# A price for the port that VectorE and GpSimd share, in the planner of a two-layer decoder trunk

## The chip, the cores and the metric

The kernel runs on one core of a Trainium2 chip. The metric is the device time of one execution in microseconds, taken as the median of several runs. The profiled execution has a time of its own, and inside it a span, from the first to the last instruction.

## The reference

The input is 1024 tokens of width 1024 in float32. Two layers follow each other, each of the form norm, mixer, residual, norm, gated feed-forward, residual:

```python
for layer in range(DEPTH):
    h = rms_norm(x, attn_norm[layer])
    if layer % 2 == 0:
        z = h @ w_in_e[i]                       # 1024 -> 2072 columns
        a_out = nsa_attention(...)              # compressed, selected and window branch, 8 heads
        b_out = swa_sink_attention(bq, bk, bv, sinks[i])   # window of 128, 8 heads
        x = x + concat([a_out, b_out]) @ w_out_e[i]
    else:
        q, k, v = split(h @ w_qkv_o[j])         # 16 heads
        x = x + dilated_attention(rope(q), rope(k), v) @ w_out_o[j]
    h = rms_norm(x, ffn_norm[layer])
    gate, up = split(h @ w_gate_up[layer])
    x = x + (silu(gate) * up) @ w_down[layer]   # hidden width 2816
return rms_norm(x, final_norm)
```

## The kernel before

The tokens are worked on in two halves of 512. Nearly every matrix product is done as three products of a high and a low part of each operand, which gives float32 accuracy from TensorE's faster formats. So each weight tile costs, beside its load, one cast on ScalarE (the high part, `splits`) and one subtraction on VectorE or GpSimd (the low part, `lows`), and each tile of attention weights costs the same (`weights`: exponential and cast on ScalarE, subtraction on VectorE or GpSimd).

The dense products (projections, output projections, feed-forward) are a list of 355 jobs that run in order on TensorE, accumulating in the banks pD. Jobs 0 to 29 are the input projection of layer 0, 30 to 116 the output projection and feed-forward of its first half and the projection of layer 1, 117 to 206 the same for the second half, 207 to 283 and 284 to 354 the two halves of layer 1. Attention runs beside them: scores in pS whose row maxima VectorE takes (`maxima`; the maxima MR are transposed by a TensorE row `pS<-ident,MR`), transposed scores in pT (`st_unit`), weights in the tiles PH, and sums in pO (`pv_unit`). 

The order of all of this isn't written by hand. Every piece of work is a generator (a task) that says which engine its next step needs, and a planner, `Kernel.run`, always advances the task whose step can start first by the planner's own clocks. One clock stands for each engine: "p" TensorE, "v" VectorE, "a" ScalarE, "g" GpSimd, "s" the DMA queue of SyncE. Each operation that is issued is priced by `account`, which sets the clock of its engine and the time from which its result is seen. The prices are `COST = {"v": (68, 1.043), "a": (50, 0.836), "g": (60, 2.2)}`, a start and an amount for each column, in nanoseconds. The order in which the planner issues is the order in which each engine's queue then runs; on the chip nothing is reordered, and real waits are set by semaphores.

Two choices lean on these clocks. `attend` lets a unit of attention go ahead of its share when the next dense row could not start in time:

```python
if n + 1 > ph["n"] * (self.done - lo) / (hi - lo):
    d = self.start(self.dense_at)
    if d <= self.clk["p"] + 250.0:
        return INF
```

And `vg` gives an elementwise operation between SBUF tiles to VectorE, unless GpSimd would be done sooner by the two clocks:

```python
v = max(self.clk["v"], self.now) + COST["v"][0] + COST["v"][1] * n
v += self.o.queue * self.waiting("v")
g = max(self.clk["g"], self.now) + COST["g"][0] + COST["g"][1] * n
return self.nc.vector if v + slack < g else self.nc.gpsimd
```

All instructions are issued through one helper, so the profile gives them all the same line, L242, and they are told apart by their tiles: S stands for the work tiles in SBUF, SM and MR for small ones, pD, pS, pT, pO for banks of PSUM.

Of the kernel before, what the change touches and what calls it, by code (L numbers as in the profile page):

```python
# [69 lines left out]
def cols(ap):  # L70
    return int(np.prod(ap.shape[1:]))


class Buf:


    def __init__(self, arena, place, raw):
        self.arena, self.place, self.raw, self.live = arena, place, raw, True
# [180 lines left out]
class Kernel:  # L259
    def __init__(self, nc, tc, ctx, io):  # L260
        self.tc, self.io = tc, io
        self.clk = {e: BEGIN for e in "pvags"}
        self.info, self.scope, self.wire, self.pe = {}, 0.0, 0.0, 0.0
        self.nc = Core(self, nc)
        pool = lambda name, **kw: ctx.enter_context(tc.tile_pool(name=name, bufs=1, **kw))
        self.const, self.sb = pool("const"), pool("sb")
        self.ps = pool("ps", space=bass.MemoryType.PSUM)
        self.dram = pool("dram", space=bass.MemoryType.DRAM)
        self.n = 0
        arena = lambda name, n, shape, dt: Arena(name, n, self.sb, shape, dt, self.info)  # L270
        self.S4 = arena("S4", N4, [P, 1032], F32R)
        self.S2 = arena("S2", N2, [P, HT], F32)
        self.PH = arena("PH", NPH, [P, HT], F16)
        self.OS = arena("OS", 3, [P, HB, 65], F32)
        self.OG = arena("OG", NOG, [P, HB, 66], F32)
        self.MR = arena("MR", 20, [P, HB], F32R)
        self.SM = arena("SM", NSM, [P, 8], F32)
        self.NM = arena("NM", 3, [HB, P], F32R)
        self.TM = arena("TM", 3, [P, HB, 64], F32)
        bank = lambda name, n, first: Arena(name, n, self.ps, [P, 512], F32, self.info, "bank", first)  # L280
        self.pS, self.pT, self.pO, self.pD = bank("pS", 2, 0), bank("pT", 2, 2), bank("pO", 1, 4), bank("pD", 3, 5)
        self.tasks, self.seq = [], 0
        self.have = {}
        self.done, self.dense_at = 0.0, None
        self.o, self.rnd, self.zone = SimpleNamespace(**ORDER), random.Random(0), 0
# [9 lines left out]
    def account(self, key, name, a, kw):  # L295

        aps = [x for x in list(a) + list(kw.values()) if hasattr(x, "tensor")]
        outs = [kw["out"] if "out" in kw else aps[0]]
        if "accum_out" in kw:
            outs.append(kw["accum_out"])  # L300
        ins = [x for x in aps if not any(x is o for o in outs)]
        t = self.clk[key]
        for x, rd in [(x, True) for x in ins] + [(x, False) for x in outs]:
            i = self.info.get(x.tensor.name)
            if i is not None:
                if rd or key != "s" or i[2] != "s":
                    t = max(t, i[1] + SELF[key] if i[2] == key else i[0])
                if not rd:
                    t = max(t, i[3])
        if key == "s":  # L310
            n = int(np.prod(a[0].shape)) * 4
            self.clk["s"] = t + 600.0
            self.last = t
            self.wire = max(self.wire, t + 1300.0) + n / 330.0
            end = see = self.wire + 700.0
        else:
            if key == "p":

                n = (4.0 if name == "matmul" else 2.0) if a[1].dtype == F32 else 1.0
                cost = max(cols(a[0]) / 2.4, 22.0) * n * (2.0 if t < COLD else 1.0) + 2.5  # L320
                t = max(t, self.pe + (26.0 if a[1].dtype in (F16, BF) else 107.0 * (n if n > 2 else 1.0)))
                self.pe = t
            else:
                c = COST[key]
                cost = c[0] + (1.45 if name == "affine_select" else c[1]) * max(cols(x) for x in aps if len(x.shape) > 1)
                if key == "a" and not any(x.tensor.name[:2] in ("pS", "pT", "pO", "pD") for x in aps):
                    cost += 43.0 if name == "copy" else 136.0
            end = t + cost
            see = end + LAT[key]
            self.clk[key] = end  # L330
            self.last = t
        for x in ins:
            i = self.info.setdefault(x.tensor.name, [0.0, 0.0, "", 0.0])
            i[3] = max(i[3], see)
        for x in outs:
            i = self.info.setdefault(x.tensor.name, [0.0, 0.0, "", 0.0])
            i[0], i[1], i[2] = max(i[0], see), max(i[1], end), key
        self.scope = max(self.scope, see)
# [2357 lines left out]
```

## Time and profile before

| | |
|---|---|
| median of 3 runs | 2660.91 us (2660.48 to 2662.5) |
| profiled execution | 2661.24 us, span 2659.2 us |
| TensorE matmul (PE) busy | 2555.7 us, 96% |
| VectorE (DVE) busy | 1882.5 us, 71% |
| ScalarE (ACT) busy | 1356.3 us, 51% |
| GpSimd (POOL) busy | 728.1 us, 27%, 513 instructions |

Busy shares are averages over stages. TensorE's idle time, and the stretches in which it was granted a lower clock, lie mostly in the first 565 us and at the starts of the later stages; between them TensorE works without a gap.

### The profile page before, as it was taken

How to read it: one execution, taken by the hardware profiler on the slowest of the kernel's cores; microseconds unless marked ns; L12 is line 12 of the kernel's file. 1: busy time of each engine (PE TensorE's matmuls, PEld its weight loads, DVE VectorE, ACT ScalarE, POOL GpSimd, SP SyncE). 2: the span in 40 equal slices, each digit the busy share in tenths (PEclk: the TensorE clock that was granted, in tenths of full speed). 3: DMA queues.
4: the chain of work that ended last, by engine and by line, in shares of the span. 5: the costliest groups of instructions: out<-in, count | busy, mean ns of one | idle time of the engine just before them, and what ended most of it. 6: DMA issues, size and time to landing. Idle time of an engine off the chain costs nothing. (4 is left out here: it accounts for less than half of the span.)

```text
span 2659.2 us, 42231 instructions
## 1 busy us (share of the span) xinstructions
PE 2555.7 (96%) x15446; PEld 1712.2 (64%) x15446; DVE 1882.5 (71%) x4266; ACT 1356.3 (51%) x2303; POOL 728.1 (27%) x513
## 2 busy tenths in 40 slices
PE   8988889999999999999999999999999999999998
PEld 7767768655555688765555688776666667654445
DVE  6888988877777775586666576687777775655554
ACT  7456555566666554344444454355556555433332
POOL 4444643210111446540000345341011114500002
PEclk9989999999999999999999999999999999999999
DMA  8665574233432345834444457954555544533320
GB/s 242 208 175 151 161 243 143 68 100 101 109 99 76 100 149 172 251 93 123 115 123 123 133 170 201 247 146 110 142 147 148 133 124 131 175 106 100 103 71 33
DMA packets 445939, 368.71 MB, mean 139 GB/s; under 512 B 54182, under 2 KB 383782, under 8 KB 445732
## 3 DMA queue, kind: packets, MB, share of 16 engines
q1 hardware_dynamic: 445732, 366.01, 48.7%
q8 instruction: 122, 2.00, 0.3%
q14 instruction: 85, 0.70, 0.1%
HBM read 298.80 MB, written 62.68 MB: 136 GB/s over the span
## 5 line engine op out<-in xcount | busy, mean ns | idle before, releaser
L242 PE MATMUL pD<-S,S 128*128 128x512 f16 (+3 forms) x9648 | 2177.5, 378 | 22.6 <-DVE S L242 15.9
L242 PEld LDWEIGHTS <-S 128*128 128x128 f16 x5376 | 509.3, 100 | 586.0 <-issue 42.3
L242 PEld LDWEIGHTS pD<-S,S 128*128 128x128 f32 x4272 | 729.3, 191 | 140.7 <-DVE S L242 5.8
L242 POOL TENSOR_TENSOR S<-S,S 128x512 f32<-128x512 f32 (+3 forms) x279 | 516.4, 1864 | 839.7 <-ACT S L242 716.4
L242 ACT ACTIVATE S<-pT 128x512 f32<-128x512 f32 (+3 forms) x304 | 171.6, 566 | 356.7 <-DVE pT L242 321.3
L242 ACT CAST S<-S 128x512 fp32r<-128x512 f32 (+2 forms) x283 | 274.1, 1020 | 154.9 <-DVE S L242 59.7
L242 DVE SCALAR_TENSOR_TENSOR S<-S,wsc,S 128x1024 f16<-128x1024 f32 x224 | 298.8, 1334 | 63.1 <-ACT S L242 62.3
L242 ACT ACTIVATE S<-S 128x1024 f16<-128x1024 f32 (+3 forms) x269 | 210.8, 784 | 142.5 <-DVE S L242 137.8
L242 ACT ACTIVATE S<-S,wsc 128x1024 f16<-128x1024 f32 x224 | 253.7, 1142 | 53.8 <-DVE wsc L242 48.5
L242 DVE TENSOR_TENSOR S<-S,S 128x512 fp32r<-128x512 f32 (+4 forms) x163 | 221.7, 1370 | 57.3 <-ACT S L242 55.1
L242 PE MATMUL pT<-S,S 128*128 128x128 f32 (+11 forms) x1072 | 255.1, 365 | 6.0 <-DMA S<-NM 3.6
L242 DVE SCALAR_TENSOR_TENSOR S<-pD,SM,S 128x512 f32<-128x512 f32 x208 | 156.2, 751 | 139.9 <-PE pD L242 130.3
L242 DVE TENSOR_TENSOR S<-pD,S 128x512 f32<-128x512 f32 (+1 forms) x238 | 156.5, 666 | 109.0 <-PE pD L242 90.8
L242 PEld LDWEIGHTS pT<-S,S 128*128 128x128 f32 (+2 forms) x1072 | 202.7, 230 | 35.9 <-DMA S<-NM 4.9
L242 DVE TENSOR_TENSOR PH<-S,PH 128x512 f16<-128x512 f32 (+3 forms) x235 | 173.6, 741 | 39.5 <-ACT PH L242 37.8
L242 POOL TENSOR_TENSOR PH<-S,PH 128x512 f16<-128x512 f32 (+2 forms) x69 | 83.4, 1210 | 418.8 <-ACT PH L242 338.3
L242 ACT ACTIVATE S<-pD,SM 128x512 f32<-128x512 f32 (+2 forms) x136 | 80.6, 605 | 200.8 <-PE pD L242 176.8
L242 ACT CAST PH<-S 128x512 f16<-128x512 f32 (+3 forms) x304 | 177.2, 587 | 10.5 <-PE pO L242 3.0
L242 PEld LDWEIGHTS <-PH 128*128 128x128 f16 (+1 forms) x3384 | 123.5, 99 | 52.8 <-issue 20.1
L242 DVE TENSOR_TENSOR pT<-pT,S 128x128 f32<-128x128 f32 (+4 forms) x176 | 91.8, 525 | 78.3 <-PE pT L242 77.5
L242 PE MATMUL pO<-S,PH 128*128 128x65 f16 (+1 forms) x3192 | 131.0, 195 | 10.6 <-DVE PH L242 8.8
L242 PE MATMUL pS<-S,S 128*128 128x256 f32 (+4 forms) x460 | 127.5, 366 | 6.6 <-DVE SM L242 3.4
(175 smaller groups left out, 1782.9 us busy)
## 6 DMA issues: line engine op xcount, KB each, us to landing
S<-in_w_gate_up SPq DMA_DIRECT2D x176, 512.0 KB
S<-in_w_down SPq DMA_DIRECT2D x88, 512.0 KB
S<-in_w_qkv_o SPq DMA_DIRECT2D x48, 512.0 KB
S<-in_w_in_e SPq DMA_DIRECT2D x22, 512.0 KB
xd<-S SPq DMA_DIRECT2D x32, 256.0 KB
S<-dhq SPq DMA_DIRECT2D x64, 128.0 KB
S<-in_w_out_e SPq DMA_DIRECT2D x16, 512.0 KB
S<-xd SPq DMA_DIRECT2D x32, 256.0 KB
```

The lines of the kernel that those rows point to most:

```text
L242: return fn(*a, **kw)
```

## The change

`account` keeps the planned start and end of the last eight GpSimd operations. A VectorE operation that touches no PSUM bank and whose planned start falls inside one of these intervals is now planned to start at the interval's end. Nothing else is edited: no instruction is added or taken out, but through the planner every engine's order can change, and so can the choices of `vg`.

```diff
-        self.info, self.scope, self.wire, self.pe = {}, 0.0, 0.0, 0.0
+        self.info, self.scope, self.wire, self.pe, self.shared = {}, 0.0, 0.0, 0.0, []
...
                 c = COST[key]
+                if key == "v" and not any(x.tensor.name[:2] in ("pS", "pT", "pO", "pD") for x in aps):
+
+                    for a, b in self.shared:
+                        if a <= t < b:
+                            t = b
                 cost = c[0] + (1.45 if name == "affine_select" else c[1]) * max(cols(x) for x in aps if len(x.shape) > 1)
...
             see = end + LAT[key]
+            if key == "g":
+                self.shared = self.shared[-7:] + [(t, end)]
             self.clk[key] = end
```

What it does to the instructions can be read from the two orders. VectorE has 4181 instructions instead of 4268 and GpSimd 605 instead of 518: `vg` sends 87 operations more to GpSimd, 35 of them subtractions of `weights`, 26 of `lows`, 8 products of `halves` (the normalised activations of the feed-forward), the others of attention's `finish` and small places. TensorE and ScalarE have the same instructions as before, 24112 and 2082, in another order. Three places show how.

First, TensorE in job 6, where layer 0's attention begins. In the order of before three transposed maxima follow each other with only scores between them (pD rows are dense ones):

```order
L242 MATMUL pD_1197<-S_15_291,S_90_1140 128x512
L242 MATMUL pS_1231<-S_86_1122,S_94_1161 128x256
L242 MATMUL pS_1231<-S_86_1122,S_94_1161 128x128
L242 MATMUL pS_1240<-ident,MR_1185 4x128
L242 MATMUL pS_1250<-S_86_1122,S_95_1176 128x256 x2
L242 MATMUL pS_1257<-S_86_1122,S_95_1176 128x256
L242 MATMUL pS_1257<-S_86_1122,S_95_1176 128x128
L242 MATMUL pS_1266<-ident,MR_1215 4x128
L242 MATMUL pS_1270<-SM_958,ones 128x1
L242 MATMUL pS_1280<-ident,MR_1253 4x128
L242 MATMUL pD_1197<-S_18_323,S_99_1244 128x512 x2
```

In the order of the change the first of them stands inside the dense rows:

```order
L242 MATMUL pS_1257<-S_92_1164,S_97_1195 128x256
L242 MATMUL pS_1257<-S_92_1164,S_97_1195 128x128
L242 MATMUL pD_1200<-S_23_360,S_89_1144 128x512 x2
L242 MATMUL pD_1200<-S_23_360,S_90_1145 128x512
L242 MATMUL pD_1265<-S_9_239,S_85_1108 128x512 x2
L242 MATMUL pD_1265<-S_9_239,S_86_1109 128x512
L242 MATMUL pS_1270<-ident,MR_1219 4x128
L242 MATMUL pD_1265<-S_13_264,S_85_1108 128x512 x2
L242 MATMUL pD_1265<-S_13_264,S_86_1109 128x512
```

Dense rows moved ahead of the row that needs VectorE's maxima.

Second, TensorE at the end of layer 0's input projection, between job 26 (rows with 408 columns) and the output projection, job 30. In the order of before four rows lie between the two:

```order
L242 MATMUL pD_4892<-S_251_4209,S_69_893 128x408
L242 MATMUL pS_4988<-S_286_4849,S_289_4882 128x256 x2
L242 MATMUL pS_4993<-ident,MR_4949 4x128
L242 MATMUL pS_5005<-S_286_4849,S_289_4882 128x256 x2
L242 MATMUL pS_5013<-ident,S_105_3993 128x128 x4
L242 MATMUL pD_5025<-S_141_2075,S_271_4611 128x512 x2
```

In the order of the change 173 rows lie between them (vcx and kc are the values and keys of the compressed branch); the stretch begins and ends so:

```order
L242 MATMUL pD_4575<-S_250_3934,S_68_879 128x408
L242 MATMUL pS_4731<-ident,MR_4617 4x128
L242 MATMUL pT_4737<-S_268_4396,kc_3164 64x512 x2
L242 LDWEIGHTS PH_4648
L242 MATMUL pO_4748<-vcx,PH_4648 128x65
```

```order
L242 MATMUL pS_5048<-ident,MR_4945 4x128
L242 MATMUL pS_5057<-ident,S_110_4283 128x128 x4
L242 MATMUL pS_5068<-S_288_4853,S_293_4875 128x256 x2
L242 MATMUL pD_5076<-S_139_1898,S_274_4608 128x512 x2
```

The last units of attention of the first half, which stood among the dense rows, now stand behind them, alone.

Third, TensorE in layer 1's first feed-forward, between job 219, the first whose input needs the whole of the new norm (`halves`), and job 220. In the order of before no attention row lies between them. In the order of the change 498 rows do, eight units of attention, of which these are the last, with job 220 behind them:

```order
L242 MATMUL pO_21219<-S_1123_20629,PH_21195 128x65
L242 MATMUL pS_21244<-ident,MR_21001 4x128
L242 MATMUL pS_21253<-ident,S_477_20968 128x128 x4
L242 MATMUL pS_21267<-S_1132_20984,S_1131_20980 128x256 x2
L242 LDWEIGHTS S_1105_20384
L242 MATMUL pD_20568<-S_1107_20414,S_1105_20384 128x512
```

They moved there from jobs 220 to 240, where dense rows now run without attention between them. Behind the warm-up of the first rows the order of before has one stretch of over 70 rows without a dense row (136 rows, at jobs 12 and 13); that of the change has eight, of 498, 248, 238, 173, 136, 131, 119 and 82 rows.

## Rows read from the trace of the kernel before

**Rows 1.** The page: busy us, share of the span, instructions.

```profile
PE 2555.7 (96%) x15446; PEld 1712.2 (64%) x15446; DVE 1882.5 (71%) x4266; ACT 1356.3 (51%) x2303; POOL 728.1 (27%) x513
```

**Rows 2.** Span and mean granted TensorE clock of the core.

```profile
core 0: 2659.2 us, clock 0.980
```

**Rows 3.** Busy time by stretch: us, then PE, PEld, DVE, ACT, POOL, clock, DMA.

```profile
0.00:374.00 374.00, 328.32 (x2231) 269.58 (x2232) 312.44 (x743) 219.54 (x436) 175.74 (x139) 0.93 0.68 195
...
1690.00:1881.00 191.00, 180.78 (x1034) 134.81 (x1033) 142.17 (x344) 100.26 (x172) 52.67 (x40) 0.95 0.63 164
1881.00:2587.00 706.00, 699.71 (x3804) 409.36 (x3803) 445.80 (x1041) 329.45 (x525) 107.74 (x79) 1.00 0.45 126
```

**Rows 4.** What PE waited for: us in total, times, longest.

```profile
PE pS L242 <- DVE MR L242: 24.6, 13, 4.9
PE pD L242 <- DVE S L242: 15.9, 10, 4.0
PE pS L242 <- DVE SM L242: 11.5, 13, 2.0
```

**Rows 5.** Timeline of 295 to 300 us: start, us, engine, operation, [idle before].

```profile
297.32 2.46 POOL L242 TENSOR_TENSOR S<-S,S 128x1024 fp32r<-128x1024 f32 x1 [1.31 <-ACT S L242]
...
297.58 2.23 DVE L242 TENSOR_SCALAR MR<-SM 128x4 fp32r<-128x4 f32 x1
...
299.86 0.37 PE L242 MATMUL pS<-ident,MR 128*4 128x128 f32 x1 [4.95 <-DVE MR L242]
```

**Rows 6.** DVE groups by form, whole span: busy us, mean ns, idle before.

```profile
L242 DVE TENSOR_TENSOR S<-pD,S 128x512 f32<-128x512 f32 x222 | 149.7, 684 | 97.3 <-PE pD L242 79.0 <-DMA S<-xd 9.9 <-ACT S L242 4.6
L242 DVE TENSOR_TENSOR PH<-S,PH 128x512 f16<-128x512 f32 x193 | 146.7, 762 | 30.6 <-ACT PH L242 29.1
L242 DVE TENSOR_TENSOR S<-S,S 128x512 fp32r<-128x512 f32 x66 | 93.4, 1428 | 41.8 <-ACT S L242 40.5 <-issue 1.1
...
L242 DVE TENSOR_TENSOR S<-S,S 128x512 f32<-128x512 f32 x44 | 48.9, 1123 | 6.1 <-ACT S L242 6.1
```

**Rows 7.** POOL groups by form, whole span.

```profile
L242 POOL TENSOR_TENSOR S<-S,S 128x1024 fp32r<-128x1024 f32 x90 | 224.0, 2493 | 135.2 <-ACT S L242 128.7 <-issue 3.4 <-DMA S<-in_w_in_e 1.2
L242 POOL TENSOR_TENSOR S<-S,S 128x512 f32<-128x512 f32 x111 | 162.2, 1472 | 223.0 <-ACT S L242 118.8 <-DVE S L242 64.7 <-PE pT L242 9.9
...
L242 POOL TENSOR_TENSOR PH<-S,PH 128x512 f16<-128x512 f32 x47 | 62.2, 1324 | 284.0 <-ACT PH L242 267.7 <-issue 16.3
```

**Rows 8.** DVE groups by form, 1240 to 1447 us, where GpSimd hardly works.

```profile
L242 DVE TENSOR_TENSOR PH<-S,PH 128x512 f16<-128x512 f32 x10 | 6.9, 687 | 2.7 <-ACT PH L242 2.6
...
L242 DVE CUSTOM_DVE_ANT_0 junk<-pS,S 128x256 bf16<-128x256 f32 x6 | 2.5, 425 | 0.9
...
L242 DVE DVE_READ_ACCUMULATOR2_ANT SM<- 128x1 f32 x24 | 2.0, 83 | 0.0
...
L242 DVE TENSOR_SCALAR MR<-SM 128x4 fp32r<-128x4 f32 x6 | 1.0, 165 | 0.1
```

**Rows 9.** PE timeline around 1907 us: one unit's sums, then scores.

```profile
1906.26 0.90 PE L242 MATMUL pO<-S,PH 128*128 128x65 f16 x24
1906.99 0.81 PE L242 MATMUL pD<-S,S 128*128 128x512 f16 x3
1907.45 2.12 PE L242 MATMUL pT<-S,S 128*128 128x128 f32 x8
1909.39 2.13 PE L242 MATMUL pD<-S,S 128*128 128x512 f16 x9
```

**Rows 10.** Around the wait of 1792.4 us, columns as in rows 3.

```profile
1792.40:1796.50 4.10, 0.05 (x2) 0.02 (x1) 4.10 (x4) 0.00 (x0) 2.81 (x1) 0.86 0.00 0
1796.50:1805.60 9.10, 8.68 (x29) 5.69 (x29) 8.13 (x20) 5.98 (x11) 2.84 (x2) 0.50 0.00 0
```

## The prediction

> **What bounds the kernel now.** The first view is the page's busy table: TensorE's matmuls are busy 2555.7 of 2659.2 us, VectorE 1882.5, GpSimd 728.1 [rows 1]. TensorE is the bound, and the change neither adds nor removes one of its instructions. [...] The mean granted clock is 0.980 [rows 2], which is 0.02 x 2659 = 53 us. That is half a microsecond of clock for each microsecond of idling, and I use this ratio below.
>
> The second view is the table by stretch. In the first 374 us TensorE has 328.3 us of work and a clock of 0.93 while VectorE is busy 312.4; from 1690 to 1881 us it is 180.8 of 191, clock 0.95; from 1881 to 2587 us 699.7 of 706, clock 1.00, with VectorE at 63% [rows 3]. So an order can lose or win in the first stage and at the starts of stages, and can win nearly nothing between them. The third view, what PE waited for, names the waits: transposed maxima for VectorE 24.6 us, dense rows for VectorE 15.9 us, further pS rows for VectorE 11.5 us [rows 4].
>
> **Is the new price true?** The timeline shows one such wait. GpSimd works from 297.32 to 299.78 us; VectorE's maxima row starts at 297.58, takes 2.23 us and ends at 299.81, and TensorE has waited 4.95 us for it [rows 5]. Where GpSimd hardly works the same row takes 0.165 us [rows 8]. Over the whole span a VectorE operation of 512 columns with one input in PSUM takes 684 ns, and the same one with both in SBUF 1428 or 1123 ns [rows 6]. VectorE does wait for GpSimd's end, and the planner of before didn't know it. The new clock "v" is nearer the truth.
>
> How much it is: 66 x (1.428 - 0.684) = 49 us, 44 x (1.123 - 0.684) = 19 us, and 193 x (0.762 - 0.687) = 14 us for the PH subtractions [rows 6, 8], together 82 us, or 0.11 us for each of GpSimd's 728 us. That is a lower bound, since smaller groups such as the maxima are left out; the wait of rows 5, 2.07 of 2.46 us, is the upper one, 0.84. I take 0.25, nearer the sum than the single case.
>
> [...]
>
> **The change, part by part.** (1) The 87 operations that go to GpSimd. A 512-column one takes 0.687 us on VectorE, and 1.324 to 1.472 us on GpSimd, one of 1024 columns 2.493 us [rows 7, 8]. VectorE is relieved of about 87 x 0.8 = 70 us and gets back 0.25 x 87 x 1.6 = 35 us of new port waits. What is left, 35 us of 1882, lies under TensorE's work wherever VectorE isn't the bound. I count it only through the instruction counts below.
>
> (2) Waits that the new order fills. Where the planner sees VectorE late, it puts dense rows ahead of the row that waits, as in job 6: three transposed maxima in a row before, and dense rows on both sides of the first one now. This bears on the 24.6 us of waits for maxima and the 15.9 us of dense rows, together 40.5 us. All of it can't be had, since every stall stays on the chip and GpSimd has more operations to cause them. Bounds: nothing, and 40.5 us with half of it again for the clock, 61 us. I take 25 us.
>
> (3) Stretches of attention without dense rows. This is the part against the change. When the planner thinks that the next dense row is late, `attend` lets units of attention go ahead; their operations come first on VectorE and delay the weights of the next dense row further, so more units follow. A stretch with attention alone can't be faster than VectorE. Six of the new stretches hold over 6 us of TensorE work each; before there is one. I cost the two clearest from rows, with 0.07 us taken off each VectorE duration because neighbours overlap.
>
> Between jobs 26 and 30 the new order has on TensorE 72 sums at 0.73 us per 24 (from 1906.26 to 1906.99, [rows 9]), 18 score rows at 0.14 to 0.24 us, 14 pS rows of the like, and 20 transposes at 0.1 us: 11 us. On VectorE it has 15 maxima pieces at 0.425 + 0.083 us, 16 operations of 512 columns at 0.687, and 34 smaller ones at 0.165 to 0.43 us [rows 8], in all 26 us, less 65 x 0.07, which is 21.4 us. GpSimd's 16 operations (14 us) add 0.25 x 14 = 3.5 us. So 24.9 us of VectorE stand against 11 us of TensorE: 13.9 us more.
>
> Between jobs 219 and 220 there are eight units: 192 sums (5.8 us), 94 score rows (eight of one unit take 1.94 us in rows 9, others less: 17 us), 28 pS rows and 12 others (6 us), about 29 us. VectorE has 99 operations, 30 of them maxima pieces (15.2 us) and some 20 of 512 columns (13.7 us), the rest small: 32.6 us after the overlap. GpSimd's 24 us add 6. So 38.6 against 28.6: 10 us. What the units fill there is a wait like that of 1792.4 us, after which the clock stood at half until 1805.6 us [rows 10]; the saving of it is in part 2.
>
> The other four, reckoned alike (VectorE with its share of GpSimd's time, against TensorE): jobs 12 to 13 25.4 against 13.1, job 38 12 against 7.5, job 131 11.2 against 6.9, job 215 16 against 13.1. The six give 13.9 + 10 + 12.3 + 4.5 + 4.3 + 2.9 = 47.9 us; the one of before gives 5.5. The difference is 42.4 us. At the edges of each stretch VectorE's work overlaps the dense rows around it, by about one operation and one wait on each side, 2 us a stretch: 42.4 - 12 = 30 us. Each is followed by dense rows at half clock as in rows 10, where 9.1 us at 0.50 lost 4.6 us; much of that falls inside the stretch, so I take 1.5 us each, 9 us. Bounds of this part: 15 us, if half is hidden, and 30 + 27 = 57 us, if the clock costs 4.6 us every time.
>
> (4) Between the stretches dense rows now run with less attention among them. They are already without gaps (699.7 of 706 us, [rows 3]), so nothing comes back there.
>
> **The sum.** Against the profiled execution's own time, 2661.24 us, which is 0.3 us above the median of the runs: 2661.2 + 30 + 9 - 25 = 2675 us.
>
> **The rivals.** The first ends on the other side: *the truer clock wins*. All three waits of rows 4 go, 52 us, with 26 us of clock, and of these 78 us two thirds are had; the stretches cost 39 us as above. 2661 + 39 - 52 = 2648 us. It decides from the point at which part 2 brings over 45 us. For it speaks that several of the longest waits sit directly behind a port stall [rows 5, 10]; against it that the stalls themselves are not removed and that GpSimd gets 17% more operations.
>
> The second: *GpSimd's results come late*. The planner prices 512 columns on GpSimd at 60 + 2.2 x 512 = 1186 ns and the trace has 1472 [rows 7]; each of the 87 moved operations is 0.29 us later than planned, 25 us in a chain of weights or norms, and nothing of part 2 is had. 2661 + 39 + 25 = 2725 us if every one is waited for, 2703 us if few are. What speaks for it is that the rows show GpSimd slower than its price; against it, that much of GpSimd's work has slack. [...]
>
> The third: *nothing that can be measured*. Stretches and filled waits cancel, as they do in my own sum but for 14 us.
>
> **How the numbers follow.** My forecast has a chance of 0.45, the late GpSimd 0.14, both slower; no change 0.16; the truer clock 0.25. 0.2%, 5.3 us, is about what a measurement of this kernel tells from no change. So faster 0.25, same 0.16, slower 0.59. The range goes from 2643 us, a little below the first rival, to 2706 us, a little above the second's milder case; the forecast's own, with the bounds of part 3 and a gain of 10 to 30 us, is 2658 to 2700 us.
>
> **What the changed profile would show.** GpSimd's busy time near 728 + 87 x 1.6 = 870 us, VectorE's below 1882. The waits for maxima below 24.6 us if part 2 is right. Between the last 408-column row and the output projection a stretch of some 25 us in which VectorE is busy over 90% and TensorE under 60%; the same, milder, before job 220, with the lower clock in both. From there to the stage's end TensorE without gaps, as before. I am wrong if TensorE's idle time falls below 103 us in spite of these stretches, or if the stretches show TensorE busy: then dense work wasn't ready there anyway, and attention took the place of idling for nothing.

## The result and the profile after

The kernel with the port price takes 2698.26 us (median of 4 runs, 2693.17 to 2703.38), the kernel before 2661.70 us beside it (2660.48 to 2663.37): a ratio of 1.0137, with an interval of 1.0117 to 1.0157. The forecast was 2675 us, so the sign was right and the loss, 36.6 us, is more than twice the 14 us expected. The profiled execution is the slowest of the runs, 2703.38 us, 42 us above the profiled execution of before; what follows accounts for these 42.

The page's busy row, beside [rows 1]:

```profile
PE 2584.3 (96%) x15446; PEld 1736.4 (64%) x15446; DVE 1829.8 (68%) x4179; ACT 1353.0 (50%) x2303; POOL 844.7 (31%) x600
```

Span and granted clock, beside [rows 2]:

```profile
core 0: 2701.5 us, clock 0.961
```

TensorE idles 2701.5 - 2584.3 = 117.2 us instead of 103.5, 13.7 more. The other 28.6 us of the loss are *busy* time: the same 15446 recorded matmuls take 2584.3 instead of 2555.7 us, while the mean clock fell from 0.980 to 0.961. It isn't the dense rows that ran slower, they average 377 ns (378 before); attention's rows in pS average 384 ns instead of 366. So two thirds of the loss is work that ran slower and one third idling. VectorE lost 52.7 us of work and GpSimd got 116.6.

What PE waited for, beside [rows 4]:

```profile
PE pT L242 <- ACT S L242: 18.2, 14, 2.8
PE pD L242 <- DVE S L242: 18.1, 10, 5.5
PE pS L242 <- DVE SM L242: 10.1, 14, 1.7
...
PE pS L242 <- DVE MR L242: 4.1, 4, 1.5
```

The waits for maxima are nearly gone, 4.1 instead of 24.6 us. Those of dense rows for VectorE are not, 18.1 instead of 15.9, and in the place of the maxima stand waits of transposed scores for ScalarE, 18.2 us where the kernel before had 3.1:

```profile
PE pT L242 <- ACT S L242: 3.1, 2, 2.2
```

Busy time by stretch, columns as in [rows 3]: the stretch between the last 408-column row and job 30, the one ahead of job 220, and the dense rows of jobs 220 to 240 behind it.

```profile
366.20:400.60 34.40, 18.60 (x125) 13.25 (x125) 23.70 (x74) 12.94 (x30) 16.01 (x16) 0.61 0.67 186
...
1822.80:1876.00 53.20, 44.00 (x327) 40.89 (x326) 35.45 (x124) 25.26 (x56) 23.63 (x23) 0.55 0.64 158
```

```profile
1876.00:1989.80 113.80, 110.50 (x525) 56.71 (x524) 66.95 (x172) 54.54 (x86) 4.68 (x5) 0.97 0.36 105
```

VectorE's busy times were forecast well, the lengths were not. In the first stretch VectorE is busy 23.7 us (forecast with its waits 24.9), but the stretch lasts 34.4, with VectorE at 69% and TensorE at 54%. In the second VectorE is busy 35.5 us (forecast 38.6), and the stretch lasts 53.2, with TensorE at 83% and a clock of 0.55.

The kernel before ran jobs 220 to 240 with these units among them:

```profile
1804.50:1946.40 141.90, 141.33 (x890) 89.70 (x889) 106.13 (x321) 80.26 (x143) 15.21 (x17) 1.00 0.56 142
```

Both windows end at the start of job 240. 141.9 - 113.8 = 28.1 us is what the eight units cost there, at clock 1.00. Alone they cost 53.2 us: 44.0 us in which TensorE is busy, and 9.2 us of idling. So some 16 of the 25 us more are the same work done slower, and 9 are waits that were covered before.

The timeline of PE inside that stretch shows it on single rows, beside [rows 9]:

```profile
1830.55 1.54 PE L242 MATMUL pO<-S,PH 128*128 128x65 f16 x24
1831.89 3.38 PE L242 MATMUL pT<-S,S 128*128 128x256 f32 x14
1835.09 1.52 PE L242 MATMUL pO<-S,PH 128*128 128x65 f16 x24
```

24 sums take 1.54 us where they took 0.90; from their start to the next row it is 1.34 us, where [rows 9] have 0.73.

To see where the time went, the next table takes the start of each job in the profiled executions. The dense rows are the same and in the same order in every kernel, so they can be counted off in each timeline. The first line is the kernel before in us, the others are differences to it. Each line is one execution, and executions of one kernel lie up to 7.5 us from their median. How much of a difference is noise can be read from price_layer1: up to job 207 its order is that of before, and yet it starts jobs 8 to 215 4.6 to 6.2 us later than the trace of before. A difference of some 6 us shows nothing by itself.

| job | 4 | 8 | 13 | 26 | 30 | 53 | 131 | 133 | 159 | 215 | 219 | 220 | 250 | 353 |
|---|---|---|---|---|---|---|---|---|---|---|---|---|---|---|
| before | 74.0 | 139.1 | 201.1 | 337.3 | 371.7 | 559.6 | 1164.3 | 1181.6 | 1332.6 | 1754.0 | 1788.3 | 1804.5 | 2020.7 | 2619.1 |
| the change | +9.2 | -5.3 | +5.3 | -2.0 | +29.0 | +22.4 | +14.3 | +32.0 | +20.8 | +13.5 | +26.9 | +71.5 | +39.7 | +42.4 |
| price_first_stage | +11.2 | -3.3 | +7.5 | -0.8 | +30.9 | +29.5 | +28.0 | +28.2 | +28.1 | +28.4 | +26.3 | +27.7 | +27.6 | +27.7 |
| price_middle | -0.7 | -1.0 | -0.9 | -1.2 | +0.2 | +2.3 | -3.6 | +13.4 | +1.9 | -6.4 | -8.2 | -6.7 | -5.5 | -7.1 |
| price_layer1 | +2.5 | +4.6 | +5.3 | +4.6 | +4.6 | +6.2 | +5.3 | +5.3 | +5.3 | +5.6 | +59.4 | +51.1 | +21.3 | +20.6 |
| not_ahead | +11.6 | -3.3 | +5.5 | -2.9 | +27.3 | +21.1 | +14.2 | +42.1 | +29.4 | +31.0 | +29.1 | +29.7 | +28.8 | +28.7 |
| order_priced | +8.8 | -7.8 | -5.8 | -15.3 | +16.5 | +20.2 | +26.2 | +41.5 | +30.0 | +23.6 | +87.5 | +79.3 | +41.4 | +41.8 |
| choice_priced | +1.5 | +11.5 | +23.3 | +22.4 | +27.8 | +32.5 | +32.7 | +37.9 | +35.6 | +28.0 | +24.4 | +25.3 | +24.6 | +26.8 |
| guarded | +0.4 | +1.1 | +2.2 | +2.5 | +2.4 | +5.5 | +0.1 | +17.0 | +5.5 | -4.8 | -6.6 | -6.5 | -7.3 | -7.1 |
| guarded_two_inputs | +0.2 | +2.2 | +3.4 | +5.2 | +5.1 | +0.9 | -6.9 | +27.0 | +11.9 | +9.1 | +7.6 | +9.7 | +8.0 | +8.1 |
| price_to_job_8 | +10.4 | -3.9 | +13.2 | +14.2 | +21.2 | +21.8 | +19.5 | +19.5 | +19.5 | +18.8 | +16.5 | +18.0 | +18.6 | +17.1 |
| price_to_job_20 | +7.8 | -7.0 | +3.6 | +9.2 | +19.6 | +19.1 | +14.2 | +15.1 | +15.0 | +13.0 | +11.5 | +13.0 | +13.2 | +13.3 |
| price_job_13_to_30 | +1.4 | +1.1 | +4.4 | +1.5 | +20.1 | +12.9 | +11.8 | +12.0 | +12.0 | +12.0 | +12.2 | +12.1 | +11.7 | +11.7 |
| price_job_20_to_30 | -0.3 | +1.3 | +1.0 | -10.7 | +5.1 | -1.1 | -1.8 | -1.8 | -1.6 | -1.3 | -0.5 | -0.7 | +0.5 | -1.0 |
| vector_price_2ns | +1.4 | +0.7 | -6.8 | -7.4 | +5.9 | +3.5 | +1.1 | +1.8 | +1.9 | +2.9 | +1.9 | +14.2 | +6.3 | +4.6 |
| scalar_price_2ns | +0.5 | +2.1 | +19.3 | +10.7 | +12.4 | +13.5 | +12.8 | +13.0 | +13.1 | +12.9 | +10.5 | +10.3 | +11.8 | +11.1 |

A difference counts only where the same work has been done: a kernel can be ahead in dense rows and behind in attention, as the change is at job 26. It is safe at jobs 53, 159, 215 and 250, where the attention of the stage is in. By these the change loses 22.4 us in the first stage, gains 8.9 from there to job 215 (22.4 to 13.5), loses 26.2 from job 215 to 250, and 2.7 later. Jobs 215 to 250 before and after:

```profile
1754.00:2020.70 266.70, 259.09 (x1592) 169.77 (x1592) 206.31 (x579) 149.26 (x263) 48.12 (x42) 0.97 0.52 132
```

```profile
1767.50:2060.40 292.90, 276.49 (x1590) 182.30 (x1590) 197.23 (x567) 149.25 (x264) 60.06 (x54) 0.88 0.47 124
```

Of the 26.2 us, 17.4 are longer busy time of TensorE and 8.8 idling.

### The profile page after: what moved, and what is told of

It is laid out like the page before. It is cut to its first block, busy times and chain, and to the rows that moved or that the text cites. A ratio compares the mean times of both kernels' runs of the same rounds, so it can differ in the third digit from the quotient of the medians.

```text
span 2701.5 us, 42329 instructions
## 1 busy us (share of the span) xinstructions
PE 2584.3 (96%) x15446; PEld 1736.4 (64%) x15446; DVE 1829.8 (68%) x4179; ACT 1353.0 (50%) x2303; POOL 844.7 (31%) x600
## 4 chain that ended last, share of the span: by engine, by line
PE 80%; DVE 5%; issue 4%; POOL 3%; DMA 3%; ACT 3%; SPq 1%; DVEq 0%; POOLq 0%; ACTq 0%
PE pD L242 66%; PE pT L242 6%; PE pS L242 5%; PE pO L242 3%; POOL S L242 3%; DVE S L242 3%; ACT S L242 2%; SPq L242 1%; DVE junk L242 1%; DMA S<-in_w_in_e 1%; DVE PH L242 1%; DMA S<-in_w_out_e 1%; DVE SM L242 1%; DVE pT L242 0%; POOL PH L242 0%
## 5 line engine op out<-in xcount | busy, mean ns | idle before, releaser
L242 PE MATMUL pD<-S,S 128*128 128x512 f16 (+3 forms) x9648 | 2162.5, 377 | 25.8 <-DVE S L242 18.1
L242 POOL TENSOR_TENSOR S<-S,S 128x512 f32<-128x512 f32 (+3 forms) x322 | 593.9, 1864 | 799.2 <-ACT S L242 694.8
L242 POOL TENSOR_TENSOR PH<-S,PH 128x512 f16<-128x512 f32 (+3 forms) x104 | 126.9, 1224 | 447.4 <-ACT PH L242 269.1
L242 PEld LDWEIGHTS pT<-S,S 128*128 128x128 f32 (+2 forms) x1072 | 204.0, 234 | 51.1 <-ACT S L242 22.9
L242 DVE TENSOR_TENSOR S<-S,S 128x512 fp32r<-128x512 f32 (+4 forms) x120 | 164.0, 1374 | 64.5 <-ACT S L242 56.8
L242 DVE TENSOR_TENSOR PH<-S,PH 128x512 f16<-128x512 f32 (+3 forms) x200 | 166.0, 834 | 38.6 <-ACT PH L242 37.3
L242 PEld LDWEIGHTS <-PH 128*128 128x128 f16 (+1 forms) x3384 | 132.6, 103 | 51.9 <-issue 18.1
L242 PE MATMUL pO<-S,PH 128*128 128x65 f16 (+1 forms) x3192 | 142.2, 201 | 13.7 <-DVE PH L242 5.3
L242 PE MATMUL pS<-S,S 128*128 128x512 f32 (+3 forms) x460 | 135.7, 384 | 13.6 <-DMA S<-dlq 4.1
```

Source lines behind the costliest of these rows:

```text
L242: return fn(*a, **kw)
```

## The experiments

Theory S: the loss sits in the stretches of attention without dense rows. Theory M: it goes with the operations moved to GpSimd (36.6 us for 87, 0.42 us each). Theory C: the lower clock sets the length of a stretch. Theory V: VectorE and the chains through it set it.

**The price in one part of the program only.** The same edit with different limits:

```diff
-                if key == "v" and not any(...):
+                if key == "v" and getattr(self, "jobi", 0) < 30 and not any(...):            # price_first_stage
+                if key == "v" and 30 <= getattr(self, "jobi", 0) < 207 and not any(...):     # price_middle
+                if key == "v" and getattr(self, "jobi", 0) >= 207 and not any(...):          # price_layer1
```

> The new price holds for jobs 0 to 29 alone. GpSimd gets 37 of the 87 extra operations; the three stretches without dense rows of the first stage (238, 119 and 173 rows) stay as in the change, the later ones are gone. Theory S (the cost sits in the stretches of attention without dense rows): in the trace of the change the jobs from 53 on start 22 us later than before, so this kernel is 18 to 26 us slower than before, about 2684 us. Theory M (the cost goes with the operations that moved to GpSimd and the port waits they make): 37/87 of 36.6 us, 16 us, about 2677 us.

Measured: 2683.59 us, ratio 1.0076 (1.0064 to 1.0089), 20 us slower.

> The new price holds for jobs 30 to 206 alone. GpSimd gets 34 extra operations; stretches of 129, 82 and 136 rows, which last for some 30 us together. Theory S: in the trace of the change the lead of before shrinks from 22.3 to 20.5 us over these jobs, so the time is within 6 us of before, 2656 to 2667 us. Theory M: 34/87 of 36.6 us, 14 us slower, 2676 us.

Measured: 2658.08 us, ratio 0.9982 (0.9973 to 0.9990), 5 us *faster*, with 34 operations moved. Theory M falls here.

> The new price holds from job 207 on. GpSimd gets only 16 extra operations, but two long stretches without dense rows arise (376 and 242 rows, where the change has 248 and 498). Theory S: some 20 us slower than before, 2676 to 2687 us. Theory M: 16/87 of 36.6 us, 7 us slower, 2669 us.

Measured: 2677.36 us, ratio 1.0050 (1.0036 to 1.0064), 14 us slower, with only 16 operations moved. 20 - 5 + 14 = 29 us of the 36.6: the parts come near the whole, and the loss lies in the first stage and in layer 1.

**No unit of attention ahead of its share while a dense row can be planned at all.**

```diff
-                        if d <= self.clk["p"] + 250.0:
+                        if d < INF:
                             return INF
```

> The price as in the change, but attention may go ahead of its share only when no dense row can be planned at all. 66 of the 87 extra operations on GpSimd remain. The stretches of the first stage remain, those at jobs 215 and 219 are gone (the longest left in layer 1 has under 71 rows; two of 139 and 138 rows arise at job 131). Theory S: the 20 us that the change loses from job 215 to job 271 are saved, 2674 to 2684 us. Theory M: 66/87 of 36.6 us stay, 28 us, 2689 us; and if attention only filled idle time there, TensorE idles instead and nothing is saved.

Measured: 2688.20 us, ratio 1.0093 (1.0079 to 1.0107), 10 us better than the change, 4 us above S's range and at M's figure. The time of the whole doesn't decide between them; the table does, by place: from job 215 to 250 this kernel loses nothing (+31.0 to +28.8) where the change loses 26.2. Only 10 us of that are left at the end because it lost 16.8 from job 131 to 215, where two new stretches stand and the change lost nothing. So the loss of layer 1 hangs on the rule that lets units go ahead. The stretch ahead of job 30 is still there (-2.9 to +27.3); no dense row could be planned then, and that rule isn't its cause.

**Extra matmuls in the two stretches, to hold the clock up.** Four bf16 products of constants of 512 columns for each score unit, into the bank that the unit then overwrites; the outputs don't depend on them.

```diff
         st = self.pT.take()
+        if self.jobi in (27, 28, 29, 220):
+            for _ in range(4):
+                nc.tensor.real.matmul(st.t, self.identB, self.mW[:, 0:512], start=True, stop=True)
```

> The order of the change, with four extra matmuls of 128x512 (bf16, about 0.216 us each at the full clock, results overwritten) ahead of each unit's scores in two stretches only: between jobs 26 and 30 (6 units, 5 us of extra work) and between jobs 219 and 220 (14 score groups, 12 us). In the change the second lasts 53.2 us with a granted clock of 0.55, PE busy 44.0 and DVE 35.5. Theory C (the stretch is long because TensorE is granted the lower clock in it, so that its 28.6 us of work take nearly twice as long): busier, it gets the higher clock, the stretch falls to 42 to 48 us and the kernel is 5 to 10 us faster than the change, about 2690 us, though it does more. Theory V (the stretch is VectorE's and the chain's length, as the prediction had it): it stays at 53 us or gets longer by up to the extra 12 us, and the kernel is at 2698 us or above.

Measured: 2709.61 us, ratio 1.0180 (1.0164 to 1.0195), 11 us slower than the change. The two stretches, columns as before:

```profile
363.50:398.30 34.80, 23.11 (x149) 14.62 (x149) 23.46 (x73) 12.67 (x30) 15.83 (x16) 0.71 0.69 183
1818.20:1881.10 62.90, 54.17 (x384) 43.52 (x381) 36.59 (x124) 25.54 (x56) 23.06 (x23) 0.76 0.54 134
```

```profile
L1628 PE MATMUL pT<-mW,identB 128*128 128x512 bf16 x56 | 18.6, 465 | 3.3 <-ACT S L242 3.2
```

The clock did rise, from 0.61 to 0.71 and from 0.55 to 0.76. The first stretch stayed as long as it was, 34.8 us: there TensorE waits, and its clock isn't what counts. In the second the units' own matmuls fell to about 54.2 - 18.6 = 35.6 us from 44.0, but the 56 added rows took 18.6, and the stretch grew by 9.7 us. The forecast of C, a shorter stretch, missed, since it left out that the remedy takes the same engine's time; that of V, a stretch longer by up to 12 us, came true. So this run alone doesn't decide for C. It shows that TensorE's work reaches the stretch's length, and that the units' own rows get shorter at the higher clock; the idling hardly changed, 8.7 us after 9.2. The next run takes V by itself.

**Extra work on VectorE instead.** Reductions of 512 columns that nobody reads, one for each score unit ahead of job 220, two for each ahead of job 30.

```diff
         st = self.pT.take()
+        for _ in range({27: 2, 28: 2, 29: 2, 220: 1}.get(self.jobi, 0)):
+            nc.vector.real.tensor_reduce(out=self.junk[:, 0:1], in_=self.mW[:, 0:512], op=ALU.max, axis=AX.X)
```

> The order of the change, with reductions added on VectorE that nobody reads: one of 512 columns for each score unit in the stretch ahead of job 220 (14 of them), two for each in the stretch ahead of the output projection (12). Each is estimated at 0.5 to 1.2 us, so 7 to 17 us and 6 to 14 us of VectorE work. The change took 53.2 us in the stretch ahead of job 220, with TensorE 83% busy at a clock of 0.55, and 34.4 us in the other, with TensorE 54% busy. Theory C (the first lasts as long as TensorE's own work does at half clock): 50 to 56 us there, as without the load. Theory V (VectorE's operations, and the chain through them, set its length, as the prediction had it): 60 to 70 us. In the stretch ahead of the output projection both expect more time, since TensorE waits there half the time: 38 to 48 us. The whole kernel: 2702 to 2712 us by C, 2708 to 2730 us by V.

Measured: 2702.01 us, ratio 1.0147 (1.0127 to 1.0168). The stretches, and the added rows (least, median and longest ns):

```profile
365.30:402.90 37.60, 19.41 (x125) 13.65 (x125) 30.55 (x86) 13.13 (x30) 15.00 (x16) 0.56 0.62 171
1823.40:1877.30 53.90, 44.56 (x327) 41.28 (x326) 44.85 (x138) 25.30 (x56) 23.85 (x23) 0.54 0.64 156
```

```profile
L1627 DVE TENSOR_REDUCE junk<-mW x26: 668/686/691, 366.8 to 1869.6; 128x1 bf16<-128x512 bf16 x26
```

Ahead of job 220, 14 x 0.686 = 9.6 us more VectorE work made the stretch 0.7 us longer, and both the stretch and the whole kernel lie in C's ranges and below V's. This decides against V there: with TensorE's added work the stretch grew, with VectorE's it didn't. Ahead of job 30, 12 x 0.686 = 8.2 us made it 3.2 us longer, a little below what both theories expected: VectorE's work lies partly on the chain there, and partly beside other waits. In the change the longest of PE's waits in that stretch is for a DMA:

```profile
PE pS L242 <- DMA S<-dlq: 4.1, 1, 4.1
```

With the reductions in, that wait is gone, and the longest sums name VectorE, 5.1 us in three waits and 3.1 in one.

**Which use of the clock does it: the order, or the choice of `vg`?** In order_priced `vg` compares a second clock of VectorE that is kept without the price; in choice_priced the order goes by the old clock and only `vg` sees the priced one.

```diff
-        v = max(self.clk["v"], self.now) + COST["v"][0] + COST["v"][1] * n
+        v = max(self.vu, self.now) + COST["v"][0] + COST["v"][1] * n                      # order_priced
+        v = max(self.clk["v"], self.vp, self.now) + COST["v"][0] + COST["v"][1] * n       # choice_priced
```

> The price moves the planner's clock of VectorE, but the choice between VectorE and GpSimd is made with a clock without it. 46 of the 87 extra operations remain on GpSimd. The order still has long stretches without dense rows (244, 209, 181 rows in and after the first stage, 145 and 135 at job 131, 374 and 284 in layer 1). Theory S (stretches): 25 to 45 us slower than before, as the change. Theory M (moved operations): 46/87 of 36.6 us, 19 us slower.

Measured: 2702.54 us, ratio 1.0147 (1.0130 to 1.0165).

> The choice between VectorE and GpSimd is made with the priced clock, but the order's own clock is the one of before. 81 of the 87 extra operations are on GpSimd. Stretches over 70 rows: 275 and 276 rows, both in the first stage; none behind it. Theory S: slower by the first stage alone, 10 to 22 us. Theory M: 81/87 of 36.6 us, 34 us slower, spread over all stages.

Measured: 2690.20 us, ratio 1.0107 (1.0090 to 1.0124). The order alone makes the whole loss, with 46 operations moved. But the choice alone loses even more in the first stage (+32.5 at job 53), more than the 10 to 22 us of S, and by another road: it is already 23.3 us late at job 13. That was the first sign that the first stage can lose under an order quite unlike that of the change.

**The price without the two places.** From job 30 on, and from job 207 on no unit ahead while a dense row can be planned:

```diff
-                if key == "v" and not any(...):
+                if key == "v" and getattr(self, "jobi", 0) >= 30 and not any(...):
...
-                        if d <= self.clk["p"] + 250.0:
+                        if d <= self.clk["p"] + 250.0 or (self.jobi >= 207 and d < INF):
```

> The price holds from job 30 on, and from job 207 on attention may not go ahead of its share while a dense row can be planned. 43 of the 87 extra operations on GpSimd; stretches as in the run with the price in jobs 30 to 206 alone (136, 129, 82, 136 rows). Theory S: the gain of that run, 5 us, and the 3 us that the run without going ahead gained behind job 207: 2653 to 2660 us, faster than before. Theory M: 43/87 of 36.6 us, 18 us slower than before, 2681 us.

Measured: 2654.86 us (12 runs, 2651.26 to 2659.16), ratio 0.9972 (0.9963 to 0.9981), 0.3% faster than the kernel before, and in S's range. How much of it the closed rule adds to the price can't be told: price_middle alone gave 0.9982 (0.9973 to 0.9990).

**The same with the price only where VectorE has two inputs in SBUF.**

```diff
-                if key == "v" and getattr(self, "jobi", 0) >= 30 and not any(...):
+                if key == "v" and getattr(self, "jobi", 0) >= 30 and len([x for x in ins if len(x.shape) > 1 and cols(x) > 1]) > 1 and not any(...):
```

> As the guarded kernel (price from job 30 on, and from job 207 on no unit of attention ahead of its share while a dense row can be planned), but the price is put only on VectorE operations with two inputs of more than one column in SBUF. GpSimd gets 23 operations more than before instead of 43. Theory S: no new stretch of over 10 us without dense rows except at job 131 (184 rows, as in the price for jobs 30 to 206), so 2650 to 2662 us, like the guarded kernel. Theory M (the loss goes with the number of operations moved to GpSimd, 0.42 us each): 2672 us.

Measured: 2666.91 us, ratio 1.0021 (1.0012 to 1.0030), 5 us above S's range and 5 below M's figure. This narrower price is slower than the broad one: from job 131 to 159 it loses 18.8 us (-6.9 to +11.9), the guarded kernel 5.4.

**Which jobs' pricing costs in the first stage?** The first edit again, with other limits on the job (below 20, 20 to 29, below 8, 13 to 29).

> The price applies only while TensorE's jobs 0 to 19 are planned; from job 20 on the plan goes by the old prices. GpSimd gets 18 operations more than before instead of 87. The long stretch without dense rows at jobs 12 to 13 is there (238 rows, as in the change), the one ahead of the output projection is not. Theory S (the first stage's loss sits in the stretch ahead of the output projection, which the price makes while the last input projections are planned): 2654 to 2668 us, since up to job 26 the full change was 2 us ahead of before. A rival (dense rows brought forward early are missing at the stage's end, so the early prices cause the loss): 2675 to 2690 us.

Measured: 2673.99 us, ratio 1.0047 (1.0035 to 1.0060).

> The price applies only while jobs 20 to 29 are planned. GpSimd gets 20 operations more than before. A stretch of 110 rows without dense rows stands ahead of the output projection, where the change has 173; the one at jobs 12 to 13 has 136 rows, as in the kernel before. Theory S: a loss of 10 to 20 us, 2672 to 2682 us, all of it between the last 408-column row and job 30's first. The rival (the early prices cause the loss): within 5 us of the kernel before, 2658 to 2668 us.

Measured: 2660.20 us, ratio 0.9995 (0.9986 to 1.0004). Theory S missed in both, and the rival, which blames the early prices, hit here and missed by 1 us above. The stretch ahead of job 30 is there, 15.8 us between jobs 26 and 30 (-10.7 to +5.1), but the dense rows that ran before it without attention had gained 10.7, and at job 53 nothing is lost. The early pricing, without that stretch, loses 19.1 by job 53.

> The port price applies only while jobs 0 to 7 are planned. GpSimd gets 3 operations more than before. One stretch of 372 rows without dense rows stands at jobs 12 to 13, none later. If the loss of the first stage comes from the pricing of the very first jobs (8 us late at job 4 in the kernel that priced jobs 0 to 19): 2668 to 2678 us; if from jobs 8 to 19: within 5 us of before.

Measured: 2674.70 us, ratio 1.0046 (1.0031 to 1.0061).

> The port price applies only while jobs 13 to 29 are planned. GpSimd gets 18 operations more than before. Stretches of 140 rows at jobs 12 to 13, 78 near job 20 and 116 ahead of the output projection. If the loss comes from the pricing of jobs 0 to 12: within 5 us of before; if from any pricing in the first stage: 5 to 20 us lost, 2667 to 2682 us.

Measured: 2672.24 us, ratio 1.0034 (1.0022 to 1.0046). Each run lies in the range that was given for a loss. Pricing jobs 0 to 7 alone costs 21.8 us by job 53, pricing jobs 13 to 29 alone 12.9: the loss belongs to no one group of jobs, and the parts don't add up.

**A price shifted by 2 ns, in the kernel before.** No port price here.

```diff
-COST = {"v": (68, 1.043), "a": (50, 0.836), "g": (60, 2.2)}
+COST = {"v": (70, 1.043), "a": (50, 0.836), "g": (60, 2.2)}      # vector_price_2ns
+COST = {"v": (68, 1.043), "a": (52, 0.836), "g": (60, 2.2)}      # scalar_price_2ns
```

> The kernel before, without the port price; only the planner's start price of VectorE is 70 ns instead of 68. No instruction is added, GpSimd gets 3 operations more. Through the planner the order still changes: the stretch of 136 rows at jobs 12 to 13 becomes two of 80 and 74, and one of 194 rows appears ahead of job 216. Theory P (the port price itself misorders the first stage): within 5 us of before by job 53, and some 5 to 10 us lost in layer 1's new stretch, 2660 to 2675 us. Theory R (any shift of the order loses in the first stage, since that of before happens to suit the chip): 5 to 30 us lost by job 53, 2670 to 2700 us.

Measured: 2665.05 us, ratio 1.0007 (0.9999 to 1.0016); +3.5 at job 53, within the noise and as theory P has it.

> The kernel before, without the port price; only the planner's start price of ScalarE is 52 ns instead of 50. GpSimd gets 4 operations more. The stretches without dense rows are one of 90 rows near job 6 and one of 331 rows at jobs 12 to 13, and none later. Theory P: within 5 us of before by job 53, 2655 to 2668 us. Theory R: 5 to 30 us lost by job 53, 2667 to 2692 us.

Measured: 2672.04 us, ratio 1.0032 (1.0020 to 1.0044); +13.5 at job 53, as theory R has it. So one of two shifts of 2 ns, which say nothing of any port, loses more than half of what the change loses in the first stage, and the other loses nothing there.

## Why the forecast was too low, point by point

**What bounds it.** Right: TensorE's idle time and its slower work are the whole loss, 13.7 + 28.6 us. Wrong was the ratio of half a microsecond of clock for each microsecond of idling. It was an estimate, 53 us from the mean clock against 2659.2 - 2555.7 = 103.5 us of idling; in what the change added it came out at two, 28.6 against 13.7. In the stretch ahead of job 220, of thin matmuls (few columns, 65 to 256), the clock was 0.55 while TensorE was busy for 83% of the time, and there it was the busy time that grew, to 44.0 us from the 28.1 that the same units cost at a clock of 1.00.

**Step 1, the 87 operations.** Right in kind. GpSimd is busy 844.7 us (forecast 870), VectorE 52.7 us less (forecast 35), and behind the first stage no run shows a cost of the moved operations themselves: 34 of them went with a gain of 5 us (price_middle), 16 with a loss of 14 (price_layer1), and choice_priced, with 25 of its 81 behind job 53, loses nothing from there on (+32.5 to +26.8). The stalls are still there. VectorE's PH subtractions even take longer, 859 against 762 ns in [rows 6] and 687 where GpSimd hardly works [rows 8], and GpSimd's 1340 against 1324 in [rows 7] (forms of the whole span after):

```profile
L242 DVE TENSOR_TENSOR PH<-S,PH 128x512 f16<-128x512 f32 x167 | 142.9, 859 | 32.8 <-ACT PH L242 32.0
```

```profile
L242 POOL TENSOR_TENSOR PH<-S,PH 128x512 f16<-128x512 f32 x73 | 97.7, 1340 | 231.9 <-ACT PH L242 202.7 <-issue 18.9 <-DVE SM L242 4.1
```

**Step 2, waits that are filled, 25 us.** The wait that it named did go: maxima fell by 20.5 us. But as a gain the term was too large and in the wrong place. The first stage, where 23.4 of the 24.6 us of these waits were, shows no gain at job 53. What is seen is in the middle of the program, 22.4 to 13.5 at jobs 53 to 215 and -7.1 us in price_middle, where the forecast had said that an order can win nearly nothing. The waits for maxima there were 1.2 us before and 1.1 after, so what shrank is others, such as pS rows for SM of VectorE, 3.7 to 0.2 us. Against part 3's own 3.8 us there (4.3 - 2 + 1.5) the 8.9 gained mean some 13 us, half of the 25.

**Step 3, stretches without dense rows.** This is the step that failed, as it put it: "So 38.6 against 28.6: 10 us". It valued the units' TensorE work at the full clock and took VectorE's time for the length. TensorE's 28.6 us was true among dense rows (28.1 by the windows), but alone these rows ran at a clock of 0.55 and took 53.2 us, of which TensorE was busy for 44.0, and VectorE's part is covered, as vector_load shows.

By place, part 3 had 11.9 us for layer 1's two stretches (10 + 2.9 - 4 + 3), and jobs 215 to 250 lost 26.2: 14 us of the 28 missing in the profiled execution. Step 2 is 12 short, 2.7 came behind job 250, and the first stage is 1.3 less than forecast: together 28. The clock's 9 us were 28.6. With the rule for going ahead closed there, the loss is gone (not_ahead, guarded).

In the first stage part 3 had 23.7 us (13.9 + 12.3 + 4.5 - 5.5 - 6 + 4.5) and 22.4 were lost, but that agreement is no proof. The stretch ahead of job 30 was forecast at 24.9 us and lasted 34.4, with neither VectorE (69%) nor TensorE (54%) at its limit; and price_job_20_to_30 shows such a stretch at no net cost, since the dense rows ahead of it had won as much.

One of the forecast's signs of being wrong came true, the stretch ahead of job 220 shows TensorE busy, but not for the reason that it gave: in not_ahead, without units there, job 220 starts 16.8 us behind job 219 (16.2 before), so dense work was ready.

**Step 4, nothing comes back between the stretches.** Right behind job 250 (39.7 to 42.4, within the noise), wrong between jobs 53 and 215, as said under step 2.

**The rivals.** The truer clock doesn't win as a whole, but on jobs 30 to 206 it does, by 5 us. Late GpSimd results are not the main cause: the profiled run's 2703 us lies at the edge of that rival's range, but by its own price of 0.29 us an operation price_layer1's 16 would have lost under 5 us and lost 14. They may be a part of it: PE's waits that name GpSimd rose from 3.9 to 12.1 us in all, and no run takes them away by themselves.

**What stays open.** Why the first stage loses some 20 us. The order of the change up to job 30 was run four times (the change, price_first_stage, not_ahead, vector_load) and came to job 30 27.3 to 31.3 us late; that of before was run five times, and came there 0 to 5.1 late. The table has eight other orders of that stage. At job 53 two of them lie within the noise (-1.1 and +3.5) and six are 12.9 to 32.5 us late; two have no port price at all, and one has it only in `vg`. So the order of before fits this chip better than most of its neighbours, and much of the first stage's loss may be no more than that it was left. How much of the 22 us the port price adds of its own can't be told from these runs.

One thing goes with the loss and wasn't tested by itself: the attention that is pulled together just ahead of job 13. Before and after, from the last dense row to job 13:

```profile
186.90:201.10 14.20, 10.11 (x85) 8.33 (x84) 11.44 (x33) 7.39 (x16) 4.44 (x5) 0.65 0.90 169
```

```profile
174.90:206.40 31.50, 22.46 (x158) 18.28 (x157) 24.74 (x71) 18.99 (x40) 10.45 (x10) 0.57 0.45 121
```

The change and the five other orders with more than 150 matmuls there (choice_priced, order_priced, price_to_job_8, price_to_job_20, scalar_price_2ns) are 13.5 to 32.5 us late at job 53. The three with fewer than 90 (price_job_20_to_30, vector_price_2ns, price_job_13_to_30) are at -1.1, +3.5 and +12.9. So theory S may hold in the first stage too, at another place than the one tested; a run that splits this stretch alone would tell.

## What to carry to other kernels

Attention in thin matmuls that ran beside dense rows cost 28.1 us here, at a granted clock of 1.00; the same rows alone cost 53.2 at 0.55, though TensorE was busy for 83% of it and waited no longer than 2.0 us at a time. Cost a stretch at the clock that it will get, and don't let a planner pull such work together to cover a wait of a few microseconds. A truer price in a greedy planner gives another order, which need not be a better one: before crediting or blaming it, shift a price by a trifle and see how far the time moves, here up to 9 us for 2 ns. Price and rule can be let in where they win: from job 30 on, with the rule closed in layer 1, the same price gives 2654.86 us.

## What the runs showed of the hardware

The granted clock was 0.55 over 53.2 us in which TensorE's matmuls are recorded busy for 44.0, and with 56 rows of 512 columns mixed in it was 0.76 over 62.9 us, busy for 54.2. So little more than half the clock was granted over a stretch in which TensorE mostly worked. Which property of these rows does it (their few columns, their f32 operands, the 9.2 us of idling in pieces) isn't told apart by these runs. In this stretch PE's longest single wait was 2.0 us, its longest sum of waits 3.2 of 53.2:

```profile
PE pT L242 <- ACT S L242: 3.2, 2, 2.0
```

VectorE's reductions of 512 columns took 668 to 691 ns, all 26 of them, in stretches where GpSimd was busy 15.0 of 37.6 and 23.9 of 53.9 us. The PH subtractions of the same width, with two inputs in SBUF, average 859 ns over the span of the change, and 687 where GpSimd hardly works [rows 8]. Whether it is the number of inputs that sets the two apart isn't shown: their types differ too. "Port" is the name that the change goes by; what in the chip makes VectorE's operations last longer beside GpSimd's isn't shown by these runs.
